# FFN 2 of a hybrid encoder layer: x sums and T1 in other pair jobs, m4's first units ahead of the first norm, the second token tile's norm behind m7's sum

## The chip, the cores and the metric

The kernel runs on one core of one Trainium2 chip. The metric is the time of one execution on the device in microseconds (us); a kernel's time is the median of its runs. The core's engines work side by side, each through its own queue in order: TensorE (PE, and PEld for its weight loads), VectorE (DVE), ScalarE (ACT), GpSimd (POOL), and SyncE (SP), which here only issues DMAs. POOL issues DMAs as well, among them those that add to what lies in the destination.

## The reference

One layer on 512 tokens of width 1024, in float32. What matters here is the last sub-layer, a gated feed-forward block (FFN 2, 2816 hidden channels) between two norms:

```
f = swiglu(rms_norm(h, ffn2_pre_g), ffn2_w1, ffn2_w3, ffn2_w2)   # (silu(x w1) * (x w3)) w2
y = h + 0.5 * rms_norm(f, ffn2_post_g)
```

In front of it stand FFN 1 of the same form, a recurrent branch and a windowed attention branch, which the change doesn't touch.

## The kernel before

**Three products.** Every float32 operand is split into hi (rounded to the type fp32r) and lo, the rest. A product is hi*hi + lo*hi + hi*lo, three matmuls. The usual split of a weight tile is one ScalarE copy for hi and one VectorE subtraction for lo (`split2`, L213 and L214; in the last stage L618 and L626). The other way makes lo by a ScalarE copy of -hi and a POOL DMA that adds the source to it (L623, L624). It spares VectorE.

**Pair jobs** (`Pairs`, L774 to L921). Most of w1 and w3 of FFN 2 is multiplied by a seven-product scheme (Strassen's, in the form with fewer sums) on 2x2 blocks, two column tiles of the weights at a time. There are 20 jobs, w1b and w3b in turn, job n for hidden tiles 2 + 2*(n//2) and the next. A job is seven groups of 12 matmuls (L768 to L770, 256 wide): a11, s1, the a22 group of the job before, s2, a12, s4, s3. While job n runs, ScalarE and VectorE split the operands of job n + 1 (`prep(n+1, 1)` to `prep(n+1, 4)`; the first is the a11 and a12 tile), and POOL makes the sums s1 to s4 of job n + 2 (L816 to L822). At fixed places of a job (`at(1)` behind the a11 group, `at(2)` behind s1, `at(3)` behind s2) hooks from the dictionary `late` run; with them the first work for w2 is put into the last jobs.

**w2 by halves** (`Halves`, L516 to L689). The first 20 tiles of the hidden layer are multiplied by w2 in the same scheme: 5 groups of 4 tiles (GS_B), and seven products in the order m1, m5, m2, m6, m3, m7, m4 (NAMES_B). Product m of group i is one unit, u = 5 * place + i: u0 to u4 are m1, u15 to u19 are m6, u20 to u24 m3, u25 to u29 m7, u30 to u34 m4. A unit has 12 matmuls (L651 to L653, 512 wide), six for each of two token tiles. `prep` makes a unit's operands: whi and wlo from the weight block (L618, L626, or L623 with L624), the split of the x part into the tile uT, or hx for the first four (L627), and then the sums that later products need in place (`sums`, L567 to L592): S is a sum or difference on x (L551), T one on weight blocks (L548). T1 of group i is b12 - b11 (`t1`), the x sum of group i (`s1`) adds two parts of the hidden layer. Both are wanted by m5 and later products; whoever comes first makes them, `sums("m1", i)` at the latest.

`step(u)` (L672) prepares up to unit u + 4 (LEAD is 5), runs the hooks of unit u, then its matmuls. Behind the last unit of m1, m5, m6 and m7, `out` moves the banks' sums; for m7 VectorE adds the bank to q5 (L663). m4 goes on accumulating in the banks of m7, so its first matmul waits until L663 has read them.

**The last stage** (`last_gemm`, L720). After units 0 to 24 the two hidden tiles left over (20 and 21) are multiplied the classical way for token tiles 0 and 1. Then come, in this order, `prep` up to unit 30, norm 0, `prep` up to unit 31, norm 1, the units of m7, the classical part of one half for token tiles 2 and 3 (12 matmuls), and the units of m4, first all five for token tile 2, its classical part and norm, then the same for tile 3. A norm (`post_norm`, L284) adds the partial sum on VectorE (L294), squares on ScalarE (L296), scales on VectorE (L297), takes the root on ScalarE (L259), then makes the output tile o in two operations of VectorE (L308), each followed by a store from SP's queue. The rows h of tiles 2 and 3, which the last norms add, are loaded by hooks of units 27 and 29 on the same queue (L701).

**What sets the order.** The whole program is issued by hand: every engine runs its instructions as the code lists them. Buffers of 512 KB come from one set of 42 (NSLOT); who takes a buffer waits for the last reader of what was in it.

Of the kernel before, what the change touches and what calls it, by code (L numbers as in the profile page):

```python
# [51 lines left out]
def hybrid_layer(ctx: ExitStack, tc: tile.TileContext, a: dict, out: bass.AP):  # L52
# [10 lines left out]
    def slot(shape, dt=F32, name="s"):  # L63
        uid[0] += 1
        return sb.tile(shape, dt, tag="slot", name=f"{name}_{uid[0]}")
# [9 lines left out]
    def f32(ap):  # L75
        return ap.bitcast(F32)
# [72 lines left out]
    def dma_to(n):  # L149
        while st["dma"] < min(n, len(order)):  # L150
            dma_one(st["dma"])
            st["dma"] += 1
# [11 lines left out]
    def split_to(n):  # L164
        while st["split"] < min(n, len(order)) and st["split"] not in paired:
            k = st["split"]
            dma_to(k + 1)
            r = raws.pop(k)
            if order[k] in BY_DMA:
                nm, i = order[k]  # L170
                pairs[k] = split_dma(r, a[nm][i * P : (i + 1) * P, :])
            else:
                hi = slot([P, D], F32R, name="whi")
                lo = slot([P, D], F32R, name="wlo")
                if order[k] in BY_POOL:
                    pool.tensor_copy(hi, r)
                else:
                    act.activation(hi, r, AF.Copy)
                dve.tensor_tensor(out=lo, in0=r, in1=f32(hi), op=ALU.subtract)
                pairs[k] = (hi, lo)  # L180
            st["split"] += 1
# [29 lines left out]
    def split2(hi, lo, src):  # L211

        act.activation(hi, src, AF.Copy)  # L213
        dve.tensor_tensor(out=lo, in0=src, in1=f32(hi), op=ALU.subtract)  # L214
# [63 lines left out]
    def bcast(name):  # L278
        t = slot([P, D], name=f"bc_{name}")
        src = a[name]  # L280
        pool.dma_start(out=t, in_=bass.AP(tensor=src.tensor, offset=src.offset, ap=[[0, P], [1, D]]))
        return t
# [233 lines left out]
    class Halves:  # L516
# [77 lines left out]
        def prep(self, n, load=True):  # L594

            G = self.G
            while self.ready < min(n, 7 * G):
                u = self.ready
                self.ready += 1
                m, i = self.names[u // G], u % G  # L600
                if load:
                    self.load(min(4 * G, 2 * G + (u if u >= U_SLOTS else u == 3) if G > 4 else 2 * G + 1 + u))
                b, odd, half = self.OPERANDS[m]
                again = m == "m3" and G > 4
                hi = self.cast.pop(i) if m == "m3" and not again else slot([P, 2, 512], F32R, name="whi")
                lo = slot([P, 2, 512], F32R, name="wlo")
                if u < U_SLOTS:
                    xs = slot([P, 2, 2, 256], F32R, name="hx")
                else:
                    xs = uT[:, :, (u + 1) % 8, :].rearrange("p e (j c) -> p e j c", j=2)  # L610
                if again:
                    split2(hi, lo, self.cast.pop(i))
                elif m == "m3":
                    act.activation(lo, f32(hi), AF.Copy, scale=-1.0)
                    pool.dma_start(out=lo, in_=self.src(b, i), accum_op=ALU.add)
                else:
                    src = self.raw[b, i]
                    act.activation(hi, src, AF.Copy)  # L618
                    if m == "m2":
                        act.activation(lo, src, AF.Copy, scale=-1.0)  # L620
                        pool.dma_start(out=lo, in_=self.src(b, i), accum_op=ALU.add)
                    elif m == "m4" and G > 4:
                        act.activation(lo, f32(hi), AF.Copy, scale=-1.0)  # L623
                        pool.dma_start(out=lo, in_=src, accum_op=ALU.add)  # L624
                    else:
                        dve.tensor_tensor(out=lo, in0=src, in1=f32(hi), op=ALU.subtract)  # L626
                split2(xs[:, 0, :, :], xs[:, 1, :, :], self.x(i, odd, half))  # L627
                self.ops[u] = hi, lo, xs
                if self.cast_at <= u < self.cast_at + G:
                    n = u - self.cast_at  # L630
                    if G > 4:
                        self.cast[n] = slot([P, 2, 512], name=f"raw_{self.nm}")
                        sp.dma_start(out=self.cast[n], in_=self.src("b22", n))
                    else:
                        self.cast[n] = slot([P, 2, 512], F32R, name="whi")
                        pool.dma_start(out=self.cast[n], in_=self.src("b22", n))
                self.sums(m, i)
# [53 lines left out]
    def blocks(nm, hid, pairs, late, h_src, gs, names, marks):  # L691

        hooks = {u: [] for u in range(7 * len(gs))}

        def tail_tile(n):
            hid.to(n + 1)
            split_to(st["get"] + n + 1)

        def h_back(t):
            h[t] = slot([P, D], name="h")  # L700
            sp.dma_start(out=h[t], in_=h_src(t))  # L701

        for at_, fn in zip(marks, (lambda n: dma_to(st["get"] + n + 1), tail_tile, h_back)):
            for n, u in enumerate(at_):
                hooks[u].append(lambda n=n, fn=fn: fn(n))
        half = Halves(nm, hid, hooks, gs, names)
        pairs.more = lambda n: half.load((LOAD_PAIRS if len(gs) == 4 else LOAD_B)[n])
        ahead = lambda: half.prep(min(half.ready + 1, U_SLOTS))
        end = len(pairs.jobs) - 1
        late[end, 1], late[end, 2 if pairs.R is None else 3] = [ahead], [ahead]  # L710
        if pairs.R is None:
            late[end - 3, 1] = [lambda: half.load(6)]
            late[end - 2, 1] = [lambda i=i: half.s1(i) for i in range(len(gs) - 1)] + [lambda: half.t1(0)]
            late[end - 1, 1] = [lambda: half.t1(1)]
            late[end - 1, 2] = [lambda: half.prep(1, False)]
            late[end, 1] = [lambda: half.t1(2)]
        pairs.run(ahead, late)
        return half

    def last_gemm(nm, hid, half, gpost_name, scale):  # L720

        tail, G, w = list(hid.seq), half.G, {}
        gpost = []
        half.hooks[GPOST_AT].append(lambda: gpost.append(bcast(gpost_name)))
        for u in range(5 * G):
            half.step(u)
        for i, k in enumerate(tail):
            w[k] = get(nm, k, ahead=len(tail) - 1 - i, rawahead=0)
        acc = {t: [half.bank["bc"][t], half.bank["bx"][t]] for t in range(2)}

        def classical(t, n, new=False):
            for k in tail:
                mm_tok(acc[t], hid[k], t, w[k], new and k == tail[0], k == tail[-1], (n,), True)

        def norm(t, ns, last=False):
            o = slot([P, D], name="o")

            def store(nn, c):
                sp.dma_start(out=out[t * P : (t + 1) * P, c], in_=o[:, c])

            post_norm(acc[t], t, gpost[0], scale * NEWT, o, store, last, part=half.part(t), ns=ns)

        for t in range(2):
            for n in range(2):
                classical(t, n)
            half.prep(5 * G + LEAD + 1 + t)
            norm(t, (0, 1))
        for u in range(5 * G, 6 * G):
            half.step(u)
        for t in range(2, 4):  # L750
            acc[t] = [half.bank["bu"][t - 2], bank("acc")]
            classical(t, 1, True)
        for t in range(2, 4):
            for u in range(6 * G, 7 * G):
                half.step(u, (t - 2,))
            classical(t, 0)
            norm(t, (1, 0), t == 3)
# [562 lines left out]
    late = {(0, 1): [lambda: keep(2 * NC1 - 1)], (1, 1): [bias_in], (2, 3): [bias_parts], (3, 1): [bias_rows]}  # L1320
# [6 lines left out]
    h.clear()  # L1327
    half = blocks("w2a", hid, pairs_a, late, lambda t: a["x"][t * P : (t + 1) * P, :], GS_A, NAMES_A, MARKS_A)
    X1 = pairs_a = late = None
# [6 lines left out]
    half = None  # L1336
# [415 lines left out]
    late = {(0, 1): [lambda: X2.update(t4=to_uT(tn[3], 0, 1)), tn.clear]}  # L1752
    pairs_b.prep(1, 1)

    half = blocks("w2b", hid, pairs_b, late, lambda t: h_scr[t], GS_B, NAMES_B, MARKS_B)
    X2 = pairs_b = None
    last_gemm("w2b", hid, half, "ffn2_post_g", 0.5)


# [27 lines left out]
LEAD = 5  # L1787
U_SLOTS = 4
LOAD_PAIRS = (0, 4, 6, 8)
LOAD_B = (0, 6, 8, 10)  # L1790
GS_A = (1, 2, 3, 4)
NAMES_A = ("m1", "m5", "m2", "m6", "m7", "m3", "m4")
MARKS_A = (14, 16, 18, 20, 22, 24), (16, 18, 20, 22, 24, 26), (24, 25, 26, 27)
# [69 lines left out]
```

## Time and profile before

| what | value |
|---|---|
| runs | 1116.06, 1116.52, 1117.1 us; median 1116.52 |
| the profiled execution | 1116.02 us, of which the profile's span is 1114.0 |
| granted TensorE clock, mean | 0.998 |
| pair jobs 15, 16, 17, 18, 19 of FFN 2 begin at (from the span's start) | about 940, 950, 960, 970, 982 us |
| the units of w2 begin at | 994 us |
| m6, m3, m7 and m4 begin at | 1035, 1049, 1068, 1087 us |

A row of the timeline gives the start, the duration, the engine and the line of the code, the operation, its tiles as out<-in, shapes, how many instructions were merged (x), and in brackets how long the engine was idle before it and what ended that. Busy time of PE is modelled at the matmul's end: matmuls overlap, so the distance of two starts tells more than a duration. A "q" behind an engine is its queue, which issues DMAs. The chain that ended last is here TensorE almost throughout.

### The profile page before, as it was taken

How to read it: one execution, taken by the hardware profiler on the slowest of the kernel's cores; microseconds unless marked ns; L12 is line 12 of the kernel's file. 1: busy time of each engine (PE TensorE's matmuls, PEld its weight loads, DVE VectorE, ACT ScalarE, POOL GpSimd, SP SyncE). 2: the span in 40 equal slices, each digit the busy share in tenths (PEclk: the TensorE clock that was granted, in tenths of full speed). 3: DMA queues.
4: the chain of work that ended last, by engine and by line, in shares of the span. 5: the costliest groups of instructions: out<-in, count | busy, mean ns of one | idle time of the engine just before them, and what ended most of it. 6: DMA issues, size and time to landing. Idle time of an engine off the chain costs nothing. (4 is left out here: it accounts for less than half of the span.)

```text
span 1114.0 us, 17982 instructions
## 1 busy us (share of the span) xinstructions
PE 1097.9 (99%) x6838; PEld 987.7 (89%) x6838; DVE 929.5 (83%) x1323; ACT 682.1 (61%) x1188; POOL 406.8 (37%) x334
## 2 busy tenths in 40 slices
PE   9999999999999999999999999999999999999996
PEld 8899999987888878899888888889999999998874
DVE  5888999999977978887778867767899897999983
ACT  7755556586757678666556664457555555568571
POOL 0143535601202413242655663011877566502010
PEclk9999999999999999999999999999999999999999
DMA  9335653467944642155222436432333233568344
GB/s 344 111 87 140 141 129 114 151 200 154 260 178 174 145 131 66 39 198 218 69 84 76 133 114 227 174 129 95 118 111 105 86 110 96 175 208 170 133 129 117
DMA packets 53349, 156.96 MB, mean 141 GB/s; under 512 B 5504, under 2 KB 7424, under 8 KB 53264
## 3 DMA queue, kind: packets, MB, share of 16 engines
q1 hardware_dynamic: 44128, 132.19, 34.7%
q0 software_dynamic: 8848, 23.12, 10.7%
q8 instruction: 53, 0.87, 0.3%
q10 hardware_dynamic: 288, 0.52, 0.1%
q14 instruction: 32, 0.26, 0.1%
HBM read 137.47 MB, written 13.62 MB: 136 GB/s over the span
## 5 line engine op out<-in xcount | busy, mean ns | idle before, releaser
L769 PE MATMUL c<-uT,wlo 128*128 128x256 f32 x516 | 146.2, 283 | 1.1 <-DVE wlo L214 1.1
L770 PE MATMUL c<-uT,whi 128*128 128x256 f32 x516 | 146.0, 283 | 0.0
L768 PE MATMUL c<-uT,whi 128*128 128x256 f32 x516 | 146.0, 283 | 0.0
L769 PE MATMUL c<-Xh,wlo 128*128 128x256 f32 x504 | 142.9, 284 | 0.7 <-DVE wlo L214 0.7
L768 PE MATMUL c<-Xh,whi 128*128 128x256 f32 x504 | 142.7, 283 | 0.0
L224 PE MATMUL f<-uT,whi 128*128 128x512 f32 (+1 forms) x368 | 136.5, 371 | 0.0
L225 PE MATMUL f<-uT,wlo 128*128 128x512 f32 (+1 forms) x368 | 134.8, 366 | 0.0
L226 PE MATMUL f<-uT,whi 128*128 128x512 f32 (+1 forms) x368 | 134.8, 366 | 0.0
L770 PE MATMUL c<-Xl,whi 128*128 128x256 f32 x456 | 129.0, 283 | 0.0
L214 DVE TENSOR_TENSOR wlo<-S,whi 128x1024 fp32r<-128x1024 f32 x86 | 118.4, 1377 | 6.0 <-POOL OL L1658 3.1
L213 ACT ACTIVATE whi<-S 128x1024 fp32r<-128x1024 f32 x86 | 88.6, 1055 | 33.5 <-DVE S L817 32.1
L769 PEld LDWEIGHTS c<-uT,wlo 128*128 128x128 f32 x516 | 99.0, 192 | 1.7 <-DVE wlo L214 1.5
L768 PEld LDWEIGHTS c<-uT,whi 128*128 128x128 f32 x516 | 99.0, 192 | 0.2
L770 PEld LDWEIGHTS c<-uT,whi 128*128 128x128 f32 x516 | 99.0, 192 | 0.0
L769 PEld LDWEIGHTS c<-Xh,wlo 128*128 128x128 f32 x504 | 96.7, 192 | 1.3 <-DVE wlo L214 1.3
L768 PEld LDWEIGHTS c<-Xh,whi 128*128 128x128 f32 x504 | 96.7, 192 | 0.3 <-issue 0.3
L652 PE MATMUL hw<-wlo,uT 128*128 128x512 f32 x220 | 86.4, 393 | 3.4 <-DMA wlo<-raw_w2b 3.2
L651 PE MATMUL hw<-whi,uT 128*128 128x512 f32 x220 | 85.9, 390 | 2.1 <-DVE hc L663 2.1
L770 PEld LDWEIGHTS c<-Xl,whi 128*128 128x128 f32 x456 | 87.5, 192 | 0.0
L653 PE MATMUL hw<-whi,uT 128*128 128x512 f32 x220 | 86.1, 391 | 0.2
L224 PEld LDWEIGHTS f<-uT,whi 128*128 128x128 f32 x368 | 69.4, 189 | 12.6 <-issue 1.7
L226 PEld LDWEIGHTS f<-uT,whi 128*128 128x128 f32 x368 | 69.4, 188 | 11.5
(440 smaller groups left out, 3180.6 us busy)
## 6 DMA issues: line engine op xcount, KB each, us to landing
raw_w2b<-in_w2b_dram SPq DMA_DIRECT2D x27, 512.0 KB, 4.5
raw_w2a<-in_w2a_dram SPq DMA_DIRECT2D x22, 512.0 KB, 4.1
raw_w1b<-in_w1b_dram SPq DMA_DIRECT2D x22, 512.0 KB, 4.2
raw_w3b<-in_w3b_dram SPq DMA_DIRECT2D x22, 512.0 KB, 4.3
raw_w3a<-in_w3a_dram SPq DMA_DIRECT2D x21, 512.0 KB, 4.3
raw_w1a<-in_w1a_dram SPq DMA_DIRECT2D x20, 512.0 KB, 4.3
raw_wg<-in_wg_dram SPq DMA_DIRECT2D x16, 512.0 KB, 4.3
h<-in_x_dram SPq DMA_DIRECT2D x8, 512.0 KB, 6.5
```

The lines of the kernel that those rows point to most:

```text
L213: act.activation(hi, src, AF.Copy)
L214: dve.tensor_tensor(out=lo, in0=src, in1=f32(hi), op=ALU.subtract)
L224: pe.matmul(ps[:, c0:c1], wh[:, s], h_, start=k == 0 and c0 == 0, stop=False, skip_group_check=True)
L225: pe.matmul(ps[:, c0:c1], wl[:, s], h_, start=False, stop=False, skip_group_check=True)
L226: pe.matmul(ps[:, c0:c1], wh[:, s], l_, start=False, stop=k == KT - 1, skip_group_check=True)
L651: pe.matmul(ps, xs[:, 0, j, c], hi[:, j, :], start=start and j == 0, stop=False, skip_group_check=True)
L652: pe.matmul(ps, xs[:, 0, j, c], lo[:, j, :], start=False, stop=False, skip_group_check=True)
L653: pe.matmul(ps, xs[:, 1, j, c], hi[:, j, :], start=False, stop=i == self.G - 1, skip_group_check=True)
L768: pe.matmul(ps, wh[:, s], xh, start=first, stop=False, skip_group_check=True)
L769: pe.matmul(ps, wl[:, s], xh, start=False, stop=False, skip_group_check=True)
L770: pe.matmul(ps, wh[:, s], xl, start=False, stop=k == 3, skip_group_check=True)
```

## The change

It has three parts, all in FFN 2.

1. In the pair jobs: the x sums of groups 0 to 3 are made in job 15 instead of job 17. The T1 of groups 0, 1 and 2 are all made in job 17, instead of one each in jobs 17, 18 and 19. The load of the first six blocks stays in job 16, the preparation of u0 in job 18.
2. lo by ScalarE copy and accumulating DMA: before, for all five units of m4. After, for m4's groups 1 and 2 (u31, u32) and for m6's groups 3 and 4 (u18, u19); m4's groups 0, 3 and 4 take VectorE's subtraction.
3. In the last stage: behind the classical part of tiles 0 and 1 the units up to 32 are prepared (so 29, 30, 31 and 32), then comes norm 0. Norm 1 comes only behind the units of m7, m7's sum and the classical part of tiles 2 and 3. u33 is prepared with the last unit of m7, as step 29 asks for it, and u34 behind norm 1, with the first unit of m4.

```
-                    elif m == "m4" and G > 4:
+                    elif G > 4 and (m, i) in BY_ADD:
                         act.activation(lo, f32(hi), AF.Copy, scale=-1.0)
                         pool.dma_start(out=lo, in_=src, accum_op=ALU.add)
...
+            late[end - 4, 1] = [lambda i=i: half.s1(i) for i in range(len(gs) - 1)]
             late[end - 3, 1] = [lambda: half.load(6)]
-            late[end - 2, 1] = [lambda i=i: half.s1(i) for i in range(len(gs) - 1)] + [lambda: half.t1(0)]
-            late[end - 1, 1] = [lambda: half.t1(1)]
+            late[end - 2, 1] = [lambda i=i: half.t1(i) for i in range(3)]
             late[end - 1, 2] = [lambda: half.prep(1, False)]
-            late[end, 1] = [lambda: half.t1(2)]
+            late[end, 1] = []
...
                 classical(t, n)
-            half.prep(5 * G + LEAD + 1 + t)
-            norm(t, (0, 1))
+        half.prep(5 * G + LEAD + 3)
+        norm(0, (0, 1))
         for u in range(5 * G, 6 * G):
             half.step(u)
         for t in range(2, 4):
             acc[t] = [half.bank["bu"][t - 2], bank("acc")]
             classical(t, 1, True)
+        norm(1, (0, 1))
...
+BY_ADD = {("m6", 3), ("m6", 4), ("m4", 1), ("m4", 2)}
```

Here end is 19, the last pair job, and G is 5.

## The prediction

> **What bounds the kernel now.** I read the page first, then who made TensorE wait in the last 264 us, where alone the change acts (its hooks begin in pair job 15, at about 940 us), then TensorE's own rows there.
>
> ```profile
> span 1114.0 us, 17982 instructions
> PE 1097.9 (99%) x6838; PEld 987.7 (89%) x6838; DVE 929.5 (83%) x1323; ACT 682.1 (61%) x1188; POOL 406.8 (37%) x334
> ```
>
> TensorE is busy 99% of the span. No matmul is added or removed, so the change can only touch the gaps between matmuls. The waits of PE from 850 us on:
>
> ```profile
> PE hw L652 <- DMA wlo<-raw_w2b: 3.2, 3, 1.2
> PE hw L651 <- DVE hc L663: 2.1, 1, 2.1
> PE c L769 <- DVE wlo L214: 1.6, 3, 0.7
> ```
>
> Three causes make 6.9 us: three waits for a lo tile that the accumulating DMA brings (m4), one for m7's sum (the hc of L663), three in the pair jobs. This view undercounts, since the end of a matmul is modelled. I therefore price them by starts:
>
> ```profile
> 1084.21 0.39 PE L244 MATMUL acc<-whi,hT 128*128 128x512 f32 x1
> 1086.66 0.47 PE L651 MATMUL hw<-whi,uT 128*128 128x512 f32 x1 [2.06 <-DVE hc L663]
> 1097.63 0.39 PE L242 MATMUL hw<-whi,hT 128*128 128x512 f32 x1
> 1098.99 0.39 PE L651 MATMUL hw<-whi,uT 128*128 128x512 f32 x1
> 1105.79 0.39 PE L242 MATMUL hw<-whi,hT 128*128 128x512 f32 x1
> ```
>
> The same 30 matmuls of m4 take 1097.63 - 1086.66 = 10.97 us for token tile 2 and 1105.79 - 1098.99 = 6.80 us for tile 3, where all operands lie ready. So **m4's waits cost 4.17 us**. 6.80 / 30 = 0.23 us is the pace of one matmul. The start of m4 comes 2.45 us after the one before it instead of 0.23: **m7's sum costs 2.2 us**. Nothing stands between these gaps and the end: what follows them is TensorE at its pace, and then tile 3's norm.
>
> **The pair jobs: x sums and T1.** The change takes the four x sums (L551) from job 17 to job 15, and the T1 of groups 1 and 2 (L548) from jobs 18 and 19 to job 17.
>
> ```profile
> 970.74 0.39 PE L769 MATMUL c<-uT,wlo 128*128 128x256 f32 x1 [0.42 <-DVE wlo L214]
> 972.97 0.39 PE L769 MATMUL c<-Xh,wlo 128*128 128x256 f32 x1 [0.54 <-DVE wlo L214]
> 981.59 0.28 PE L768 MATMUL c<-uT,whi 128*128 128x256 f32 x1
> 982.52 0.39 PE L769 MATMUL c<-uT,wlo 128*128 128x256 f32 x1 [0.66 <-DVE wlo L214]
> ```
>
> ```profile
> 963.73 3.58 DVE L551 TENSOR_TENSOR hEO<-hEO,hEO 128x512 f32<-128x512 f32 x4
> 967.23 1.21 DVE L548 TENSOR_TENSOR raw_w2b<-raw_w2b,raw_w2b 128x1024 f32<-128x1024 f32 x1
> 978.05 1.21 DVE L548 TENSOR_TENSOR raw_w2b<-raw_w2b,raw_w2b 128x1024 f32<-128x1024 f32 x1
> 981.25 1.21 DVE L214 TENSOR_TENSOR wlo<-raw_w3b,whi 128x1024 fp32r<-128x1024 f32 x1
> ```
>
> Job 17: from 963.73 the sums hold VectorE to 967.23, the T1 to 968.4. Of these 3.5 us about 1.1 are a collision with POOL, as below, which the first operation there meets in any case. In their place stand three T1 of 1.14 each: 1.1 + 3.4 = 4.5 us, to 968.25. The a11 lo behind them is 0.1 earlier, so the waits at 970.74 and 972.97 all but stay. Gain 0.1.
>
> Job 18: the T1 at 978.05 is gone, and the lo that PE wants at 981.71 starts at about 980.0 instead of 981.25 and ends before PE comes. The wait at 982.52 goes: 0.93 us after the start before it instead of the 0.12 at which the 256 wide matmuls follow each other (949.88 to 950.00, below), so 0.8, and 0.1 more because the first matmul after a wait takes 0.39 instead of 0.28. Gain 0.9. Without the T1 in job 19 too, the next preparations wait for ScalarE instead, so this lead goes no further.
>
> Job 15: is there room for the sums?
>
> ```profile
> 941.21 0.68 DVE L214 TENSOR_TENSOR w<-raw_w3b,w 128x512 fp32r<-128x512 f32 x1
> 946.51 1.62 DVE L214 TENSOR_TENSOR wlo<-raw_w1b,whi 128x1024 fp32r<-128x1024 f32 x1 [4.62 <-ACT whi L213]
> ```
>
> ```profile
> 941.37 1.68 POOL L821 TENSOR_TENSOR S<-raw_w3b 128x512 f32<-128x512 f32 x1 [4.43 <-DVE cc L891]
> 945.76 1.30 POOL L817 TENSOR_TENSOR S<-raw_w3b,raw_w3b 128x512 f32<-128x512 f32 x1
> ```
>
> ```profile
> 949.88 0.28 PE L768 MATMUL c<-uT,whi 128*128 128x256 f32 x1
> 950.00 0.28 PE L769 MATMUL c<-uT,wlo 128*128 128x256 f32 x1
> ```
>
> VectorE is idle for 4.62 us, but POOL runs its four sums there, of about 1.3 us each. In 963.73 the first x sum, beside a POOL operation, took 1.7 us, and the other three 0.6 each (3.5 in all). If the two engines take turns, the four x sums end at 941.8 + 4 x (1.3 + 0.45) = 948.8, and the a11 lo of job 16, 1.14 later, just after 949.9, where PE wants it at 950.00: with the release and the slow first matmul a new wait of 0.2 us. Alone they would take 2.4 and cost nothing; were each of the four 0.5 later still, the wait would be 2.2. I take 0.2, nearest to the collision that the row shows, and job 16 has room for the rest. The Trainium skill, SBUF — State Buffer, Who interferes with whom, says that a VectorE instruction with two SBUF inputs and a GpSimd instruction that reads SBUF block each other for a whole instruction; the trace agrees (1.7 against 0.6 us). Without that rule the sum would be 0.2 us better. Pair jobs: 0.1 + 0.9 - 0.2 = **0.8 us gained**.
>
> **m6 by accumulation.** For u18 and u19 (m6's groups 3 and 4) the lo leaves VectorE and becomes a ScalarE copy and a POOL DMA.
>
> ```profile
> 1040.53 1.22 DVE L626 TENSOR_TENSOR wlo<-raw_w2b,whi 128x1024 fp32r<-128x1024 f32 x1
> 1035.21 1.07 ACT L618 ACTIVATE whi<-raw_w2b 128x1024 fp32r<-128x1024 f32 x1 [4.88 <-PE hw L652]
> 1064.67 1.06 ACT L623 ACTIVATE wlo<-whi 128x1024 fp32r<-128x1024 f32 x1
> 1066.03 0.86 POOL L624 DMA_DIRECT2D wlo<-raw_w2b  x1 [6.88 <-ACT wlo L623]
> DMA to landing us min/median/max: 4.4/8.6/8.8
> 1046.35 0.39 PE L652 MATMUL hw<-wlo,uT 128*128 128x512 f32 x1
> 1049.36 0.50 PE L653 MATMUL hw<-whi,uT 128*128 128x512 f32 x1
> ```
>
> VectorE saves 2 x 1.14 = 2.3 us from the operation at 1040.53 on; it has no idle time up to 1068. So m3 is prepared earlier, and the short wait at 1049.36 goes (0.06 over the pace, 0.1 behind it): 0.2 us. The cost is a deadline. u19's whi starts at 1035.21, when u14 has given up a buffer; 1.0 + 1.0 later both copies are made, POOL issues 0.3 after that (1064.67 + 1.06 to 1066.03), at 1037.5. u18's whi was made before u19's, so its DMA goes first. PE wants the lo at 1046.35. A landing of 4.4 to 5.7 us, as the two that ran without the others took, leaves 3 us; one of 8.8, as the three that ran among each other and two h loads took, leaves nothing. Beside u19's run one or two loads of SP. I take no wait; the other end is in the rivals. ScalarE has room for the copies, 4.88 us before this whi alone. All of this moves with PE, so the 0.8 us from above change nothing.
>
> **The end: units first, norm 1 later.**
>
> ```profile
> 1059.16 1.06 ACT L618 ACTIVATE whi<-raw_w2b 128x1024 fp32r<-128x1024 f32 x1 [2.15 <-DVE wlo L626]
> 1071.94 1.28 ACT L259 ACT_TABLE_LOAD   x1
> 1068.92 0.70 DVE L294 TENSOR_TENSOR hc<-hw,hc 128x512 f32<-128x512 f32 x1
> 1076.75 0.68 DVE L294 TENSOR_TENSOR hc<-hw,hc 128x512 f32<-128x512 f32 x1
> 1080.65 1.42 DVE L308 SCALAR_TENSOR_TENSOR o<-fg,r,h 128x512 f32<-128x512 f32 x2
> 1085.22 0.69 DVE L214 TENSOR_TENSOR uT<-hEO,uT 128x512 fp32r<-128x512 f32 x1 [1.87 <-ACT uT L213]
> 1085.83 1.28 DVE L663 TENSOR_TENSOR hc<-hw,hc 128x512 f32<-128x512 f32 x2
> ```
>
> Before, m7's sum stands behind norm 1 (1076.75 to 1082.0) and behind two preparations whose ScalarE part, queued behind that norm, came late. After, VectorE does units 29 to 32 first: one lo more (u30, 1.14) and two more splits of 0.6, that is 2.3 us, against 0.8 + 2.3 from above. So norm 0 starts near 1068 instead of 1068.92 and ends near 1075 (5.2 us by norm 1's rows, up to 1.4 more for its table load at 1071.94); u33 follows till 1077. PE ends m7 at about 1080.7 (before, 11 matmuls of 0.23 ahead of 1084.21, so 1081.7; less 1.0), so the sum runs 1080.4 to 1081.7, while PE does the 12 matmuls of the tails of tiles 2 and 3 until 1083.4. The sum is in time: 2.2 us gained.
>
> m4's units: u30 is split on VectorE; ScalarE's whi of u27, held at 1059.16 until VectorE gave up a buffer, comes 3 us earlier, at 1056; four units of 1.5 (1.0 and 0.5) lead to u31, whose two copies are made by 1064, those of u32 2.5 later, by 1066.5: issued 0.3 after these, they land by 1076 even at 8.8 us; u33 is ready at 1077. **u34** is the late one, queued on ScalarE and VectorE behind norm 1. That norm has 1081.7 + 5.2 = 1087.0; u34's lo and split end at 1088.2 and 1088.8. PE, from 1083.4 with 24 matmuls in front, comes at 1088.8 and wants the lo at 1089.1, the split at 1089.3. In time by half a microsecond: 4.2 us gained. Of norm 1 itself only two stores wait, and SP's queue gains by it:
>
> ```profile
> 1082.52 0.92 SPq L701 DMA_DIRECT2D h<-h_scr  x2
> ```
>
> The two h loads stood behind norm 1's stores, and ran beside m4's DMAs; now they are issued ahead of these stores.
>
> **Sum.** 0.8 + 0.2 + 2.2 + 4.2 = 7.4 us. The profiled execution took 1116.02 us around its span of 1114.0, 0.5 under the median of 1116.52; 1116.5 - 7.4 = **1109.1 us**.
>
> **Rivals.** (1) *The accumulated lo lands late in m6.* For: ScalarE works in order, and the copies need buffers that earlier units give up; u18's lo is wanted 12 matmuls before u19's, at 1043.6. Should its buffer come only with u14's end at 1035.2, a copy of 1.0, an issue 0.3 later and 8.8 us make 1045.3, 1.7 late, and u19 behind it may add 0.8: 2.5 us, 1111.6. Against: two landings of 4.4 and 5.7. The Trainium skill, SBUF — State Buffer, SBUF: two separate sides, speaks for it: VectorE can keep GpSimd from writing the descriptors of its DMAs. No run here shows it: POOL's issue takes 0.86 at 1066.03, with VectorE busy.
> (2) *Norm 1 takes the place of the wait.* With 1.4 us more, as norm 0's table load had, u34 is 0.9 late; with a late buffer, 2: 1110 to 1111. Against: the table is loaded once.
> (3) *It doesn't do what it says:* m7's sum stays behind something on VectorE, as u33's preparation if ScalarE gets its buffer late, and 2.2 are kept: 1111.3.
> (4) *Slower.* The lo buffers of u18 and u19 come free late. Copy, issue and 8.8 us make 10.1, as in (1), against 1043.6. A buffer that comes at 1033.5 costs nothing, one that comes at 1040.9 eats the whole 7.4, and one that waits for u17 (1043.4) makes it 9.9: 1116.5 + 2.5 = 1119.0. Against: u19's whi got u14's buffer at 1035.21, five units ahead.
>
> **Chances.** Forecast 0.60, (1) 0.14, (2) 0.08, (3) 0.04; of (4), 0.07 for a loss that about eats the gain and 0.07 for more. Faster by over 0.2% (2.2 us, about what a measurement of this kernel can tell from no change) 0.86, within 0.2% 0.07, slower 0.07. The range: below, the 1.5 us of the waits at 970.74 and 972.97 and the 0.2 of job 15 might go as well, 1107.4, so I start at 1107.3. Above, (1), (2) and (3) end at 1111.6, and two of them together, or job 15's wait of 2.2, give 1113.0.
>
> **What would show it.** The row of waits "hc L663" gone, and no L652 wait for wlo<-raw_w2b of m4; m4's first 30 matmuls in 6.8 us. The wait at 982.52 gone, those at 970.74 and 972.97 still there; a short new one at about 950 for the a11 lo. No wait at u18 and u19. Wrong would be: L652 waiting for wlo<-raw_w2b near 1043 to 1047 (rivals 1 and 4), or L652 or L653 waiting near 1089 for VectorE (rival 2), or a wait at 950 well over 0.2.

## The result, and the profile after

The changed kernel takes 1109.98 us (median of 5 runs, 1108.97 to 1112.62), the kernel before 1116.06 beside it; the ratio is 0.9947, 95% interval 0.9932 to 0.9961. That is 6.1 us faster. Forecast were 1109.1 us, a range of 1107.3 to 1113.0, and 0.86 for faster. The profiled execution took 1108.97 us around a span of 1107.2 (1116.02 and 1114.0 before).

The span and the busy times from the page, then the waits of TensorE from 850 us on (who waited for whom: us in total, times, longest):

```profile
span 1107.2 us, 17988 instructions
PE 1096.0 (99%) x6838; PEld 987.7 (89%) x6838; DVE 934.2 (84%) x1324; ACT 680.1 (61%) x1187; POOL 407.0 (37%) x333
```

```profile
PE hw L652 <- DMA wlo<-in_w2b_dram: 1.1, 1, 1.1
PE c L770 <- DVE wlo L214: 0.8, 2, 0.5
```

(The change adds a line of code, so L769 of the kernel before is L770 here.) Both rows that carried the forecast are gone, that of m7's sum (L663) and that of the lo tiles of m4 (wlo<-raw_w2b). Two of the three waits in the pair jobs are left. One row is new in the list: u14, the last unit of m2, waits for its lo, which the other accumulating DMA brings, from DRAM. It was there before, but too short to be listed.

By distances of starts (pace 0.23 us, and 0.12 in the pair jobs, as in the prediction) TensorE lost 9.2 us from 900 us on before the change and 2.7 after it:

| wait | before | after |
|---|---|---|
| pair jobs, at 970 and 973 | 1.48 | 1.33 |
| pair jobs, at 982 | 0.91 | 0 |
| u14's lo | 0.36 | 1.35 |
| first unit of m3 | 0.18 | 0 |
| m7's sum | 2.30 | 0 |
| lo of m4's units | 4.00 | 0 |

TensorE's rows at the first matmul of m4, at the classical part behind its first 30 matmuls, and at u14:

```profile
1084.03 0.39 PE L651 MATMUL hw<-whi,uT 128*128 128x512 f32 x1
1090.83 0.39 PE L242 MATMUL hw<-whi,hT 128*128 128x512 f32 x1
1032.44 0.50 PE L652 MATMUL hw<-wlo,uT 128*128 128x512 f32 x1 [1.07 <-DMA wlo<-in_w2b_dram]
```

The DMA that brings u14's lo, with its size and the time from issue to landing, after the change and then before it:

```profile
wlo<-in_w2b_dram POOLq DMA_DIRECT2D x1, 512.0 KB, 8.7
```

```profile
wlo<-in_w2b_dram POOLq DMA_DIRECT2D x1, 512.0 KB, 7.7
```

The 30 matmuls take 6.80 us, as the same 30 of tile 3 always did; before it was 10.97.

VectorE in the pair jobs:

```profile
941.70 6.88 DVE L551 TENSOR_TENSOR hEO<-hEO,hEO 128x512 f32<-128x512 f32 x4
948.51 1.21 DVE L214 TENSOR_TENSOR wlo<-raw_w1b,whi 128x1024 fp32r<-128x1024 f32 x1
963.62 4.58 DVE L548 TENSOR_TENSOR raw_w2b<-raw_w2b,raw_w2b 128x1024 f32<-128x1024 f32 x3
979.88 1.21 DVE L214 TENSOR_TENSOR wlo<-raw_w3b,whi 128x1024 fp32r<-128x1024 f32 x1
```

The four x sums take 6.88 us in job 15, beside POOL's four sums, where 2.4 would do alone (7.0 were worked out). The lo behind them ends at 949.72; TensorE wants it here at 949.90, and has it. The three T1 take 4.58 us (4.5). The lo of job 19 starts at 979.88 (980.0).

VectorE in the last stage:

```profile
1069.20 0.69 DVE L214 TENSOR_TENSOR uT<-hEO,uT 128x512 fp32r<-128x512 f32 x1 [1.85 <-ACT uT L213]
1069.81 0.68 DVE L294 TENSOR_TENSOR hc<-hw,hc 128x512 f32<-128x512 f32 x1
1080.83 1.37 DVE L663 TENSOR_TENSOR hc<-hw,hc 128x512 f32<-128x512 f32 x2 [2.68 <-PE hw L653]
1087.35 1.22 DVE L626 TENSOR_TENSOR wlo<-raw_w2b,whi 128x1024 fp32r<-128x1024 f32 x1
1088.48 0.69 DVE L214 TENSOR_TENSOR uT<-hEO,uT 128x512 fp32r<-128x512 f32 x1
```

m7's sum now waits for TensorE, 2.68 us, instead of TensorE for it. u34's lo and split, behind norm 1, end at 1088.57 and 1089.17. u34 begins 24 matmuls after 1084.03, at 1089.5: in time by about a microsecond.

POOL's issues of the accumulating DMAs, their landing, and SP's queue:

```profile
1032.35 0.90 POOL L624 DMA_DIRECT2D wlo<-raw_w2b  x1 [7.43 <-ACT wlo L623]
1037.50 0.85 POOL L624 DMA_DIRECT2D wlo<-raw_w2b  x1 [4.25 <-ACT wlo L623]
1066.38 0.84 POOL L624 DMA_DIRECT2D wlo<-raw_w2b  x1 [8.52 <-DVE wlo L626]
1068.94 0.85 POOL L624 DMA_DIRECT2D wlo<-raw_w2b  x1 [1.73 <-ACT wlo L623]
DMA to landing us min/median/max: 5.5/5.5/8.2
```

```profile
1075.78 1.00 SPq L739 DMA_DIRECT2D out_dram<-o  x2
1076.87 0.91 SPq L701 DMA_DIRECT2D h<-h_scr  x2
1086.80 1.00 SPq L739 DMA_DIRECT2D out_dram<-o  x2
```

The first two are u18 and u19 of m6; even at 8.2 us u18's lo is there at 1040.5 and wanted at 1043.4. The other two, for m4, are issued 8 to 10 us before the h loads, and overlap each other without harm.

### The profile page after: what moved, and what is told of

Same layout as the page of the kernel before. It is cut to its first block, busy times and chain, and to the rows that moved or that the text cites. A ratio compares the mean times of both kernels' runs of the same rounds, so it can differ in the third digit from the quotient of the medians.

```text
span 1107.2 us, 17988 instructions
## 1 busy us (share of the span) xinstructions
PE 1096.0 (99%) x6838; PEld 987.7 (89%) x6838; DVE 934.2 (84%) x1324; ACT 680.1 (61%) x1187; POOL 407.0 (37%) x333
## 4 chain that ended last, share of the span: by engine, by line
PE 89%; DVE 6%; ACT 3%; DMA 1%; issue 1%; DVEq 0%; SPq 0%; ACTq 0%
PE c L770 12%; PE c L771 12%; PE c L769 12%; PE f L224 9%; PE f L226 9%; PE f L225 9%; PE hw L652 5%; PE hw L653 5%; PE hw L651 5%; PE acc L244 1%; PE acc L242 1%; PE acc L243 1%; DVE wlo L214 1%; PE pt L1623 1%; DMA wlo<-in_w2b_dram 1%
## 5 line engine op out<-in xcount | busy, mean ns | idle before, releaser
L770 PE MATMUL c<-uT,wlo 128*128 128x256 f32 x516 | 146.1, 283 | 0.3 <-DVE wlo L214 0.3
L769 PE MATMUL c<-uT,whi 128*128 128x256 f32 x516 | 146.0, 283 | 0.0
L770 PE MATMUL c<-Xh,wlo 128*128 128x256 f32 x504 | 142.9, 284 | 0.7 <-DVE wlo L214 0.5
L769 PE MATMUL c<-Xh,whi 128*128 128x256 f32 x504 | 142.7, 283 | 0.0
L770 PEld LDWEIGHTS c<-uT,wlo 128*128 128x128 f32 x516 | 99.0, 192 | 0.7 <-DVE wlo L214 0.5
L769 PEld LDWEIGHTS c<-uT,whi 128*128 128x128 f32 x516 | 99.0, 192 | 0.2
L770 PEld LDWEIGHTS c<-Xh,wlo 128*128 128x128 f32 x504 | 96.7, 192 | 1.2 <-DVE wlo L214 1.2
L769 PEld LDWEIGHTS c<-Xh,whi 128*128 128x128 f32 x504 | 96.7, 192 | 0.3 <-issue 0.3
L652 PE MATMUL hw<-wlo,uT 128*128 128x512 f32 x220 | 86.0, 391 | 1.2 <-DMA wlo<-in_w2b_dram 1.1
```

Source lines behind the costliest of these rows:

```text
L652: pe.matmul(ps, xs[:, 0, j, c], lo[:, j, :], start=False, stop=False, skip_group_check=True)
L769: pe.matmul(ps, wh[:, s], xh, start=first, stop=False, skip_group_check=True)
L770: pe.matmul(ps, wl[:, s], xh, start=False, stop=False, skip_group_check=True)
```

## The experiments

Times are medians of 5 runs, of 11 for the first two and the last; "before" is the kernel before on the same chip. What TensorE lost is worked out from starts as above.

**1. The pair jobs' part alone.** The kernel before with this edit:

```
+            late[end - 4, 1] = [lambda i=i: half.s1(i) for i in range(len(gs) - 1)]
...
+            late[end - 2, 1] = [lambda i=i: half.t1(i) for i in range(3)]
...
+            late[end, 1] = []
```

> The kernel before with the pair jobs' part alone (x sums in job 15, T1 of groups 0 to 2 in job 17). My theory: it is worth the wait of job 19's first lo and little else, 0.9 to 1.1 us in TensorE's rows: 1115.1 against 1116.06. In its profile the wait at 982 is gone, those at 970 and 973 stay, none at 950; m7's sum still costs about 2.2 us and the first 30 matmuls of m4 about 11 us. Rival: VectorE, freed of T1 in the last two jobs, is ahead through all of w2, so that m7's sum comes earlier too; then 2 us or more.

1115.06 against 1116.24; ratio 0.9989 (0.998 to 0.9998). TensorE's waits:

```profile
PE hw L652 <- DMA wlo<-raw_w2b: 2.9, 3, 1.3
PE hw L651 <- DVE hc L663: 1.7, 1, 1.7
PE c L769 <- DVE wlo L214: 0.8, 2, 0.5
PE hw L652 <- DMA wlo<-in_w2b_dram: 0.7, 1, 0.7
```

The pair jobs' row falls from three waits to two, 1.6 to 0.8 us; the end keeps both of its waits. 1.2 us, as the theory said. The interval of that time, 0.2 to 2.2 us, doesn't exclude the rival by itself, but the rows do: by starts m7's sum still costs 1.95 us (2.3 before) and m4's lo tiles 3.75 (4.0 before). Even that small gain need not come from the pair jobs, since u14's wait is 0.9 us here instead of 0.36 (experiment 10 shows the same effect).

**2. The last stage's order alone.** The changed kernel with the hooks of the pair jobs as before, and with lo by DMA for all of m4 and none of m6:

```
-BY_ADD = {("m6", 3), ("m6", 4), ("m4", 1), ("m4", 2)}
+BY_ADD = {("m4", i) for i in range(5)}
```

> The kernel before with the last stage's new order alone: units up to 32 ahead of norm 0, norm 1 behind m7's sum, but the pair jobs as before and lo by accumulating DMA for all of m4 and for nothing of m6. My theory: m7's sum is in time (2.2 us gained) and u30 to u33 land early (their waits gone), but u34's DMA is issued behind norm 1, at about 1089, and lands 4.4 to 8.8 us later, while TensorE wants it at about 1090: a wait of 3 to 7 us. 1112.7 to 1116.9, likeliest 1114. Rival: the order alone is the whole gain and which units use the DMA doesn't matter: 1110.

1114.60 against 1116.24; ratio 0.9983 (0.9974 to 0.9993). The waits, then the issue of u34's DMA and the landing of all five:

```profile
PE hw L652 <- DMA wlo<-raw_w2b: 2.4, 1, 2.4
PE c L770 <- DVE wlo L214: 1.6, 3, 0.7
```

```profile
1089.14 0.86 POOL L624 DMA_DIRECT2D wlo<-raw_w2b  x1 [8.34 <-ACT wlo L623]
DMA to landing us min/median/max: 4.4/4.9/8.2
```

m7's sum is in time and four of m4's units are. One wait remains, of u34, 2.4 us (3 to 7 expected): issued behind norm 1 it landed quickly, 4.4 us later, at 1093.6. In this profile the granted clock fell to 0.5 at about 1094.5 us, for 3 us (mean of the run 0.996), which cost about 1.5 us more. It fell 0.9 us after this wait; whether the wait brought it is not shown by a single profile.

**3. m6's lo by subtraction again.** The changed kernel with `BY_ADD = {("m4", 1), ("m4", 2)}`.

> The changed kernel with m6's lo all by VectorE's subtraction again (m4 as in the change). My theory: the 2.3 us of VectorE that come back cost the short wait at m3's first unit, 0.2, and nothing at the end, since there VectorE waited for ScalarE in front of norm 0 (1.85 us idle at 1069): within 0.5 us of the changed kernel, 1110.2. Rival: this room on VectorE is what puts m7's sum and u33 in time; then 1 us or more is lost.

1109.52 against 1116.24; ratio 0.9933 (0.992 to 0.9947): the same as the changed kernel. No wait at m3, at m7's sum or in m4. VectorE's first row of norm 0 and m7's sum:

```profile
1071.42 0.68 DVE L294 TENSOR_TENSOR hc<-hw,hc 128x512 f32<-128x512 f32 x1
1081.90 1.37 DVE L663 TENSOR_TENSOR hc<-hw,hc 128x512 f32<-128x512 f32 x2 [2.14 <-PE hw L653]
```

TensorE runs 1.07 us later here than in the changed kernel, and norm 0 starts 1.6 later: the 2.3 us of VectorE cost 0.5 in front of norm 0, and m7's sum still has 2.14 us to spare. **m6's accumulation brings nothing that can be seen here.** Whether it is worth the 0.2 at m3 stays open. The wait at m3 depends on u14's: it is 0.28 us in experiment 2 (u14 0.27), but gone in experiment 10, where neither the pair jobs nor m6 are touched and u14 waits 1.24. TensorE then comes later to m3, and u14 waits 1.1 us in this run too.

**4. Norm 1 back in its old place**, directly behind norm 0; everything else as changed:

```
         half.prep(5 * G + LEAD + 3)
         norm(0, (0, 1))
+        norm(1, (0, 1))
...
-        norm(1, (0, 1))
```

> The changed kernel with norm 1 directly behind norm 0, ahead of m7's units, as before; the units up to 32 stay prepared ahead. My theory: most of m7's wait came from the preparations that stood between norm 1 and the sum, and from ScalarE's copies for them. With those gone norm 1 ends near 1082, u33 follows, the sum ends near 1084 where TensorE wants it at 1083.2: about 0.7 us lost, 1110.7. Rival: norm 1's place is worth the full 2.2 us: 1112.2. If it costs nothing the move of norm 1 is idle.

1108.78 against 1116.24; ratio 0.9928 (0.9916 to 0.9941). VectorE at the end of norm 1, u33's preparation and m7's sum, then TensorE's first matmul of m4:

```profile
1079.22 1.42 DVE L308 SCALAR_TENSOR_TENSOR o<-fg,r,h 128x512 f32<-128x512 f32 x2
1080.55 1.22 DVE L626 TENSOR_TENSOR wlo<-raw_w2b,whi 128x1024 fp32r<-128x1024 f32 x1
1081.69 0.69 DVE L214 TENSOR_TENSOR uT<-hEO,uT 128x512 fp32r<-128x512 f32 x1
1082.29 1.28 DVE L663 TENSOR_TENSOR hc<-hw,hc 128x512 f32<-128x512 f32 x2
```

```profile
1083.12 0.47 PE L651 MATMUL hw<-whi,uT 128*128 128x512 f32 x1
```

The sum's first half ends at 1082.9, and m4 starts 0.1 late. **Norm 1's move costs and brings nothing by itself**: with the units prepared ahead there is room for both norms in front of m7's sum. There is nothing to spare, though: VectorE goes from norm 1 to the sum without a pause. The expected 0.7 set the norms at about the changed kernel's times against a TensorE that wants the sum at 1083.2. In this run TensorE wanted it at 1083.0, but norm 0 started 1 us earlier than in the changed kernel too (1068.79 for 1069.81), as u14's wait was 0.30 for 1.35.

**5. Units prepared late.** The changed kernel with `half.prep(5 * G + LEAD + 1)`: units 29 and 30 alone ahead of norm 0.

> The changed kernel, but only units 29 and 30 are prepared ahead of norm 0; u31 to u33 come with the units of m7. My theory: the DMAs of u31 and u32 are then issued behind norm 0's root, at about 1076.5 and 1079, land 4.4 to 8.8 us later, and are wanted at 1084.8 and 1086.2: up to 0.5 and 1.7 us late, 0 to 2 us lost, likeliest 0.5: 1110.5. If the landing takes 8.8 us here too, 1112. Rival: to prepare m4 ahead is the heart of the change; then 3 to 4 us are lost.

1109.32 against 1116.28; ratio 0.9933 (0.992 to 0.9947), no wait in m4. The two issues for u31 and u32, and the landing of all four in that kernel:

```profile
1074.22 0.84 POOL L624 DMA_DIRECT2D wlo<-raw_w2b  x1 [16.72 <-ACT wlo L623]
1076.78 0.85 POOL L624 DMA_DIRECT2D wlo<-raw_w2b  x1 [1.72 <-ACT wlo L623]
DMA to landing us min/median/max: 6.9/8.0/8.6
```

They run beside the h loads, take up to 8.6 us, are there by 1085.4, and no matmul waits. So this half of the new order isn't needed either, as long as norm 1 is late.

**6. T1 spread out.** The changed kernel with T1 of group 0 in job 16, group 1 in job 17, group 2 in job 19:

```
+            late[end - 3, 3] = [lambda: half.t1(0)]
-            late[end - 2, 1] = [lambda i=i: half.t1(i) for i in range(3)]
+            late[end - 2, 1] = [lambda: half.t1(1)]
...
-            late[end, 1] = []
+            late[end, 1] = [lambda: half.t1(2)]
```

> The changed kernel with T1 of group 0 in job 16 (behind its s2 group), of group 1 in job 17 and of group 2 in job 19. My theory: the two waits left in the pair jobs, at 970 and 973, are there because three T1 stand ahead of job 18's first lo; one fits into VectorE's idle 1.1 us at 957 in job 16, one into the idle time of job 19, so that lo comes 2.3 us earlier and both waits, 1.3 us together, go: 1108.7 against 1110.0. Rival: the two lo are late because they collide with POOL's sums, whatever stands ahead of them: within 0.3 us of the changed kernel.

1107.80 against 1116.28; ratio 0.992 (0.9906 to 0.9935). The waits, and the one T1 left in job 17 with the two lo tiles behind it:

```profile
PE hw L652 <- DMA wlo<-in_w2b_dram: 0.9, 1, 0.9
```

```profile
964.72 2.31 DVE L548 TENSOR_TENSOR raw_w2b<-raw_w2b,raw_w2b 128x1024 f32<-128x1024 f32 x1
967.66 1.23 DVE L214 TENSOR_TENSOR wlo<-raw_w1b,whi 128x1024 fp32r<-128x1024 f32 x1 [0.63 <-ACT whi L213]
968.88 2.25 DVE L214 TENSOR_TENSOR wlo<-S,whi 128x1024 fp32r<-128x1024 f32 x1
```

Both pair job waits are gone. The first lo starts at 967.66, before POOL's next sums begin, and now waits for ScalarE itself. The collision only takes place behind it. So the theory holds and the rival falls.

**7. u14's lo by subtraction:**

```
-                    if m == "m2":
+                    if m == "m2" and (G == 4 or i < 4):
```

> The changed kernel with the lo of u14 (the last unit of m2) by VectorE's subtraction instead of the accumulating DMA from DRAM. My theory: the wait of 1.35 us in front of u14 is that DMA's landing (8.7 us after its issue, behind a hc copy and a buffer), and VectorE, which has m6's operands ready 4 us ahead, can take 1.14 us more: 1108.7 against 1110.0. Rival: VectorE is the next bound; its queue passes the delay on to m6 and m3, and nothing is gained or up to 1 us lost.

1108.04 against 1116.28; ratio 0.9922 (0.9909 to 0.9934). The only row of waits left:

```profile
PE c L770 <- DVE wlo L214: 0.8, 2, 0.5
```

The wait in front of u14 is gone and none came at m6 or m3: the theory holds.

**8. Both.**

> The changed kernel with both: T1 spread over jobs 16, 17 and 19, and u14's lo by subtraction. My theory: all waits of TensorE left in FFN 2 go, 2.6 us: 1107.4 against 1110.0. Rival: less than the sum of the two single edits, as VectorE's lead is spent twice.

1107.02 (1106.01 to 1108.04) against 1116.28; ratio 0.9913 (0.99 to 0.9926): the fastest of all, 9.3 us under the kernel before and about 3 under the changed one. No wait of TensorE is listed from 850 us on, and by its starts nothing is lost from 900 us on. The span is 1105.1 us. The rival (less than the sum of both) is not settled by the times: the single edits took 2.2 and 1.9 us off the changed kernel's median, and both together 3.0, with intervals of about 1.5 us to each side. By starts nothing is missing, since the two waits of 1.33 and 1.35 us are both gone.

Experiments 4 and 5 each undo one half of the new order, and each cost nothing. So what holds the gain?

**9. The old order with the new choice of lo.** Both halves undone, the pair jobs and BY_ADD as changed.

> The changed kernel with the last stage in its old order (units 29 and 30, norm 0, unit 31, norm 1, then m7), but with the new choice of who makes lo, and the new pair jobs. The two halves of the new order each made up for the other's absence. Theory now: they do the same thing, they keep norm 1 and the preparations for m4 from standing in one row ahead of m7's sum. With neither, norm 1 ends near 1081, u32 (by DMA) and u33 come behind it, m7's sum is 1.5 to 2 us late as before, and u32's DMA, issued near 1082 beside the h loads, lands 8.5 us later, 4 late: 4 to 6 us lost against 1110.0, 1114 to 1116. Rival: the choice of who makes lo is the gain, and the order is worth nothing: 1110 to 1111.

1111.71 against 1116.10; ratio 0.9961 (0.9948 to 0.9973).

```profile
PE hw L652 <- DMA wlo<-raw_w2b: 1.3, 1, 1.3
PE c L769 <- DVE wlo L214: 0.8, 2, 0.5
PE hw L652 <- DMA wlo<-in_w2b_dram: 0.5, 1, 0.5
PE hw L651 <- DVE hc L663: 0.3, 1, 0.3
```

By starts m7's sum costs 0.5 and u32's lo 1.6 us. So with the new split the order is worth about 2 us of the 6.1 (1.7 by the medians), less than the 4 to 6 expected, and more than the rival's nothing. The 2.6 us that the lo tiles of u33 and u34 had cost are gone without any new order.

**10. The h loads ahead**, alone, in the kernel before:

```
-MARKS_B = (17, 18), (20, 22), (21, 22, 27, 29)
+MARKS_B = (17, 18), (20, 22), (21, 22, 23, 24)
```

> The kernel before with one edit of its own: the h loads of token tiles 2 and 3 hang on units 23 and 24 instead of 27 and 29, so that they stand in SP's queue ahead of the norms' stores and not beside m4's accumulating DMAs. Theory: these DMAs take 8.6 us instead of 4.4 to 5.6 because of the two h loads; without them u32 and u33 land in time and u34 about 0.6 late: m4's wait of 4 us falls to 0.6, m7's sum stays late by 2.2 us: 1112.8 against 1116.2. Rival: they take 8.6 us because three of them are in flight at once, whatever SP does: within 1 us of 1116.2.

1113.23 against 1116.10; ratio 0.9974 (0.9965 to 0.9983). The landing of the five accumulating DMAs, SP's queue, and TensorE's waits:

```profile
DMA to landing us min/median/max: 4.4/4.5/6.0
```

```profile
1052.33 9.61 SPq L701 DMA_DIRECT2D h<-h_scr  x4
1075.03 7.58 SPq L739 DMA_DIRECT2D out_dram<-o  x4
```

```profile
PE c L769 <- DVE wlo L214: 1.6, 3, 0.7
PE hw L651 <- DVE hc L663: 1.4, 1, 1.4
PE hw L652 <- DMA wlo<-in_w2b_dram: 1.0, 1, 1.0
```

The median landing falls from 8.6 to 4.5 us, and **the whole wait of m4 is gone**, with all five units still by DMA, the norms in their old places and nothing prepared ahead. The rival (three DMAs in flight slow each other) falls: these three are issued 2.6 us apart, each overlaps the next, and they take 4.4 to 4.6 us. But u34's lo lands only 0.28 us before TensorE comes for it (1092.25 against 1092.53), and TensorE comes that late because m7's sum still costs 1.65 us. With that sum in time, u34's DMA, issued behind norm 1 as before, would be late again, by about 1.4 us.

## Why the prediction was right, and where it wasn't

**The terms.** m4's wait (4.2 forecast, 4.0 measured by starts), m7's sum (2.2, and 2.3), m3's first unit (0.2, and 0.2), job 19's lo (0.9, and 0.9) and the two other pair jobs (0.1, and 0.15) all came out at the size that was said; why m3's wait went is open (experiment 3). Their sum less the one new term, u14, is the 6.5 us that TensorE's rows gained; span and time fell by 6.8 and 7.1 in the profiled executions. The step that made no wait where 0.2 was allowed is job 15: the x sums ended 0.2 us earlier than worked out (948.58, not 948.8) and TensorE came 0.1 earlier, so the lo was just in time. The collision itself was read rightly: 1.7 us for an x sum beside POOL, four times over. The Trainium skill, SBUF — State Buffer, Who interferes with whom, says why (both instructions read SBUF through a shared port, and one blocks the other), and the trace agrees: 6.88 us for four that need 2.4 alone.

**The term that failed: u14's lo.** "All of this moves with PE" was too simple. The chain in front of u14 did move with PE (POOL issued 1.15 us earlier), but its DMA landed 8.7 us after its issue instead of 7.7. In the ten profiles in which this DMA exists, u14's wait lies between 0.27 and 1.35 us, and it follows no edit: 0.30 in experiment 4 and 1.35 in the changed kernel, which are alike up to there; 1.24 in experiment 10 and 0.36 in the kernel before, alike as well. So about 1 us differs from profile to profile, with one profile of each program: whether from execution to execution or from program to program, these can't tell. That is as much as the distance between the forecast 1109.1 and the measured 1110.0, though it is not shown for runs without a profile. A load of SP runs beside this DMA, issued 1.8 us behind it, and takes long when the DMA does (6.4 us before, 7.1 after, 7.0 in experiment 10); whether it makes the spread wasn't tried.

**Causes that were argued and don't hold as told.** The sum for m4 was right, but the prediction put the 4.2 us down to preparing ahead and to making u33 and u34 by subtraction, and told of SP's queue only as a side effect. Experiment 10 shows that in the kernel before this side effect was the larger part: SP's queue held the h loads back behind norm 1's stores (at 1082.52), so that they ran beside the last three accumulating DMAs and made 8.6 us of 4.5. It is not the only cause, since in experiment 10 the late m7 sum still covers for u34's late issue. The change works on the wait in several ways at once: it issues the h loads before norm 1's stores, issues two of the DMAs long before, and takes two others away. The first alone, with m7's sum late, left nothing of the 4.0 us (experiment 10), and the last alone left 1.6 (experiment 9). Without the last, the other two leave u34's wait (experiment 2). Beside the new split, either half of the new order is enough (experiments 4 and 5). The early issue by itself wasn't tried. In the same way m7's sum is in time with norm 1 in its old place. And m6's accumulation, for which 0.2 was reckoned, shows no gain: in the changed kernel VectorE spends the room waiting for ScalarE in front of norm 0 (1.85 us at 1069.20), and without the room (experiment 3) it doesn't wait there and norm 0 starts only 0.5 us later. ScalarE was late there because u28's whi, too, had to wait for a buffer (until 1059.52, 1.24 us idle, released by a matmul of L652), so norm 0 started at 1069.81 and not at 1068.

**The rivals.** A late lo in m6 (1 and 4) didn't come: the landings were 8.2 and 5.5 us, 2.8 and about 3 us before they were wanted, and though ScalarE stood idle for 2.3 us ahead of u18's second copy, probably for its buffer (the profile names nothing that ended it), that copy started at 1031.0, before the point (1033.5) from which it would have cost anything. The starvation that the Trainium skill describes for VectorE's operations in a two-port mode (SBUF — State Buffer, SBUF: two separate sides) is not what slows these DMAs: in experiment 10 they take 4.5 us and in the kernel before 8.6, with the same work on VectorE. What agrees is another sentence of the Trainium skill, in Trainium Kernel Development and Optimization, Key Constraints: DMAs from SP's, ScalarE's and POOL's queues run on the same 16 engines and interleave. Norm 1 in place of the wait (2) missed by the microsecond that u34 had to spare; rival (3) is refuted by the 2.68 us that m7's sum now waits for TensorE. As for the range, job 15's wait of 2.2 us alone would have made 1111.1, not 1113.0; only two rivals together reach that end.

## What to carry to other kernels

Where TensorE is at 99%, price a change by the distances of its starts, gap by gap; the sum of a few named gaps was right to within a microsecond here. Such a sum holds only when all its gaps close together: while one stays open, it can hide another behind it, as m7's sum hid u34's late lo in experiment 10. But a gap that closes doesn't say which edit closed it: undo the parts one at a time, and both of a pair together, before believing in any. And where a transfer takes longer in one place than in another, look first at what else moves bytes at that moment, and at whose queue put it there: one line that hung two loads on earlier units gained 2.9 us by itself, where the whole change gained 6.1.

## What the runs showed of the hardware that was not expected

An accumulating DMA of 512 KB from SBUF to SBUF lands 4.4 to 4.6 us after its issue even with another of its kind in flight (experiment 10), and in m4 8.2 to 8.8 us when the h loads, plain loads of 512 KB from SP's queue, run beside it (the kernel before and experiments 1, 2, 5 and 9). And VectorE and POOL took turns so evenly that a count was enough: four x sums, each ending about 0.5 us behind one POOL operation of 1.6 to 1.7 us, 6.88 us where 7.0 were reckoned.
